# A list scheduler given the tensor engine's drain at a change of array division, and a longer assumed delay before products

## The chip, the cores and the metric

The kernel runs on one core of one Trainium2 chip. The metric is the device time of one execution in microseconds; the median of three runs stands for a kernel. The core has a tensor engine (PE in the rows; its weight loads are PEld), a vector engine (DVE), a scalar engine (ACT), GpSimd (POOL) and a queue that issues all DMAs (SP).

## The reference

One layer of a streaming encoder over 512 tokens of width 1024, in float32. Three token mixers run side by side on one input projection, their results are gated and summed, and a feed-forward block follows:

```
h = rmsnorm(x, norm_mix)
y_a = rwkv7_mixer(h @ wi[:, :OFF_HGRN], ...)          # 16 heads of 64
y_b = hgrn2_mixer(h @ wi[:, OFF_HGRN:OFF_SSM], ...)   # 8 heads of 128
y_c = mamba2_mixer(h @ wi[:, OFF_SSM:OFF_GATE], ...)  # 4 groups of 8 heads
gates = sigmoid(h @ wi[:, OFF_GATE:])                 # 3 x 1024 columns
merged = sum of gates[branch] * (y_branch @ wb[branch])
x = x + merged @ w_out
gate, up = split(rmsnorm(x, norm_ffn) @ w_ffn_in)
out = rmsnorm(x + (silu(gate) * up) @ w_ffn_out, norm_final)
```

## The kernel before

Every dense product is computed in three passes on values split into a high and a low part (`mm3`: high by high, high by low, low by high), so each weight tile that arrives by DMA is first cast by the scalar engine (`wh`, `rgh`, `gwh`) and then subtracted by the vector engine (`wl`, `rgl`, `gwl`) in `wcols`. There are three such streams: w (tiles `wr`, `wh`, `wl`), rg and gw. The normed input lies in `hh` and `hl`.

The mixers work in small pieces. The RWKV-7 mixer goes over eight pairs of heads: `r_stage1` (projections into bank `rd`, decay, the score products `SB` and `KAo`), `r_inverse` (a forward substitution of 31 steps on the vector engine, tiles `Yq` and `tmpI`, then small products) and `r_chain` (products into bank `ru`, each evacuated by the scalar or the vector engine before the next). Their products are 64 rows by 64 columns: `quads` lays four of them into quarters of the 128x128 array. The HGRN2 mixer goes over eight heads with seven levels of decay; `blocks` makes sixteen products of 128 rows by 32 columns into bank `m`. The Mamba-2 mixer works on four groups, in two streams. The gates (bank `g`, 24 tiles of 128 columns, `gates`) depend on `hh` and `hl` alone, and so do the other dense projections; these are what the tensor engine does between the pieces of the mixers. At the end `merge_early` takes two of the three branch products and `tail` does the rest: merge, output projection and feed-forward block, all in products over the full array.

What sets the order is the class `Recorder`. The kernel's instructions are not issued but recorded with what they depend on, a duration and a priority (0 RWKV chain and front, 1 next RWKV pair and all weight loads, 2 HGRN, 3 Mamba, 4 gates, 5 early merge, 6 tail). `flush` then runs a list scheduler: it steps through time, takes the engine that can start next, and gives it the instruction of the lowest priority number, and among these the first recorded, of those that are ready by then. The order found is emitted per engine (line 402 for all instructions, so rows of this kernel are told apart by tiles, not by lines). Its tables are three:

- `cost` and `passes`: durations. For a product `passes` returns the load of the weights, the passes, and which of the sixteen 32x32 parts of the array it uses; `self.pe` holds when each part has its weights and when it ends.
- `lat`: what lies between the end of one instruction and the start of one that depends on it.
- `port`, `parts`, `switch`: smaller rules for the vector and scalar engines.

Products in different parts of the array overlap in this model, and a change from full to divided use of the array costs nothing in it but the wait for the parts. The delay from a scalar or vector instruction to a product is:

```python
            if eng == "tensor":
                return 0.17 if e == "scalar" else 0.15
```

Of the kernel before, what the change touches and what calls it, by code (L numbers as in the profile page):

```python
# [74 lines left out]
class Queue:  # L75


    def __init__(self, rec, name):
        self.rec, self.name = rec, name
# [5 lines left out]
class Recorder:  # L85
# [6 lines left out]
    def __init__(self, tc):  # L92
        self.tc, self.nc = tc, tc.nc
        for e in self.ENGINES:
            if e != "gate":
                setattr(self, e, Queue(self, e))
        self.ops, self.done = [], 0
        self.prio = 0
        self.writes, self.reads, self.acc = {}, {}, {}
        self.gate, self.tiles_dram = {}, set()  # L100
        self.tiles, self.proto, self.views = [], {}, set()
        self.tags, self.prev, self.before, self.dead = {}, {}, {}, set()
        self.free = dict.fromkeys(self.ENGINES, 0.0)
        self.table = None
        self.dma = 0.0

        self.pe, self.pe_last = [[(0.0, 0.0)] * 4 for _ in range(4)], 0.0
        self.parts = {}
        self.port = {"vector": 0.0, "gpsimd": 0.0}

# [91 lines left out]
    def passes(self, out, method, args):  # L202


        n = 1
        for d in out.shape[1:]:
            n *= d
        load = args[1].shape[-1] / 1200
        if method == "transpose" or args[1].dtype == F32R:
            ps = [n / (1200 if method == "transpose" else 2226)]  # L210
        else:
            ps = [n / 1200] * 2
        rows, cols = ((q[1] // 32, -(-q[2] // 32)) for q in (self.region(args[1]), self.region(out)))
        return load, ps, [(i, j) for i in range(*rows) for j in range(*cols)]

    def shares(self, eng, method, args, kw, out):

# [84 lines left out]
    def flush(self):  # L302
        ops, lo, n = self.ops, self.done, len(self.ops)
# [4 lines left out]
        now = {e: [] for e in self.ENGINES}  # L308

        def lat(j, eng):  # L310
            e = ops[j][0]
            if e == eng:
                return {"vector": 0.13, "sync": 2.0, "tensor": -0.3}.get(e, 0.0)
            if e == "sync":
                return 1.0 if ops[j][9] > 0.5 else 2.05
            if e == "gate":
                return 0.0
            if eng == "tensor":
                return 0.17 if e == "scalar" else 0.15
            return 0.21 if e == "tensor" else 0.14  # L320

        def push(k):
# [2 lines left out]
        for k in range(n - lo):  # L325
            op = ops[lo + k]
            for j in op[5]:
                if j >= lo:
                    succ[j - lo].append(k)
                    need[k] += 1  # L330
                else:
                    ready[k] = max(ready[k], ops[j][8] + lat(j, op[0]))
            if not need[k]:
                push(k)
        order, left = [], n - lo
        while left > len(order):
# [10 lines left out]
            t, e = best  # L347
            while fut[e] and fut[e][0][0] <= t:
                k = heapq.heappop(fut[e])[1]
                heapq.heappush(now[e], (ops[lo + k][6], k))  # L350
            k = now[e][0][1]
            if e == "scalar" and self.switch(ops[lo + k]) and ops[lo + k][6] and t - ready[k] < 3:
                c = [x for x in now[e] if not self.switch(ops[lo + x[1]])]
                if c:
                    k = min(c)[1]
            now[e].remove((ops[lo + k][6], k))
            heapq.heapify(now[e])
            op = ops[lo + k]
# [3 lines left out]
                order.append(-1 - lo - k)  # L362
                left += 1
            if e == "tensor":
                load, ps, parts = op[9]
                loaded = max([ready[k]] + [self.pe[i][j][0] for i, j in parts])
                end = max(self.pe[i][j][1] for i, j in parts)
                for d in ps:
                    loaded = self.pe_last = max(loaded + load, end + 0.003, self.pe_last + 0.006)
                    end = loaded + d  # L370
                for i, j in parts:
                    self.pe[i][j] = (loaded, end)
                op[4] = end - t
# [17 lines left out]
            for m in succ[k]:  # L391
                ready[m] = max(ready[m], op[8] + lat(lo + k, ops[lo + m][0]))
                need[m] -= 1
                if not need[m]:
                    push(m)
# [1239 lines left out]
```

## Time and profile before

| | us |
|---|---|
| median of three runs | 1689.2 |
| lowest and highest run | 1685.62, 1690.41 |
| the profiled execution, whole | 1685.3 |
| its span, first to last instruction | 1683.2 |
| tensor engine busy in the span | 1645.2 |
| vector engine busy | 1021.6 |
| scalar engine busy | 832.6 |

The profiled execution is 2.1 us longer than its span and lies 3.9 us under the median of the runs. The span has two parts: up to about 1240 us the mixers with dense products between them, and from there the tail. A product's row gives its start and a duration that includes its way through the pipeline, so the distance from one start to the next tells what a product costs, and the idle time in brackets, with what ended it, is what the engine stood still. An idle time under 0.15 us is not printed.

### The profile page before, as it was taken

The numbers are of one execution on the slowest core, as the hardware profiler recorded it, in microseconds if no ns is written. First come the engines' busy times: TensorE is split into PE (matmuls) and PEld (weight loads), VectorE is DVE, ScalarE is ACT, GpSimd is POOL, SyncE is SP. The second block draws the span as 40 slices with busy tenths as digits, with TensorE's granted clock in tenths as the row PEclk, the third lists the DMA queues.
The fourth block names the chain that finished last, engine by engine and source line by source line (L and its number), as shares of the span: only waits on it lengthen the run. The fifth ranks groups of instructions, "written<-read, shape, count | busy, mean of one in ns | idle before, by whom it ended". The sixth has DMA issues, their size and how long they took to land. (4 is left out here: it accounts for less than half of the span.)

```text
span 1683.2 us, 32033 instructions
## 1 busy us (share of the span) xinstructions
PE 1645.2 (98%) x12302; PEld 1330.7 (79%) x12302; DVE 1021.6 (61%) x2327; ACT 832.6 (49%) x1518; POOL 270.3 (16%) x285
## 2 busy tenths in 40 slices
PE   7999999999999999999999999999999999999998
PEld 6887787787887777879688797777888888888886
DVE  5777878787878787884846647443353533333233
ACT  6665645657647455465755745324433433333222
POOL 1212323313223211120302103010020000000000
PEclk9999999999999999999999999999999999999999
DMA  5342333333334233433454545866572333333332
GB/s 169 80 104 62 97 80 78 78 89 78 83 74 106 70 95 82 108 89 106 124 156 118 146 126 176 280 201 202 158 219 76 113 94 94 94 94 94 96 99 75
DMA packets 291321, 192.08 MB, mean 114 GB/s; under 512 B 59054, under 2 KB 255048, under 8 KB 291168
## 3 DMA queue, kind: packets, MB, share of 16 engines
q1 hardware_dynamic: 291167, 190.04, 40.0%
q8 instruction: 96, 1.57, 0.4%
q14 instruction: 58, 0.47, 0.1%
HBM read 164.22 MB, written 25.76 MB: 113 GB/s over the span
## 5 line engine op out<-in xcount | busy, mean ns | idle before, releaser
L402 DVE TENSOR_TENSOR wl<-wr,wh 128x512 fp32r<-128x512 f32 x267 | 189.7, 711 | 244.1 <-ACT wh L402 234.9
L402 ACT CAST wh<-wr 128x512 fp32r<-128x512 f32 x267 | 164.8, 619 | 308.3 <-PE d L402 148.1
L402 DVE TENSOR_TENSOR rgl<-rgr,rgh 128x512 fp32r<-128x512 f32 x142 | 100.7, 710 | 139.0 <-ACT rgh L402 137.8
L402 ACT CAST rgh<-rgr 128x512 fp32r<-128x512 f32 x142 | 87.9, 619 | 195.6 <-PE rd L402 89.9
L402 PE MATMUL d<-hh,wh 128*128 128x512 f32 (+1 forms) x424 | 171.7, 405 | 0.4 <-DVE q L402 0.4
L402 PE MATMUL d<-hh,wl 128*128 128x512 f32 (+1 forms) x424 | 168.7, 398 | 1.1 <-DVE wl L402 1.1
L402 PE MATMUL d<-hl,wh 128*128 128x512 f32 (+1 forms) x424 | 169.0, 399 | 0.0
L402 PE MATMUL rd<-hh,rgh 128*128 128x512 f32 (+1 forms) x324 | 130.8, 404 | 3.1 <-DVE k L402 1.4
L402 PE MATMUL rd<-hh,rgl 128*128 128x512 f32 (+1 forms) x324 | 129.4, 399 | 0.0
L399 ACT ACT_TABLE_LOAD x100 | 128.3, 1283 | 1.7
L402 PE MATMUL rd<-hl,rgh 128*128 128x512 f32 (+1 forms) x324 | 129.1, 398 | 0.0
L402 PEld LDWEIGHTS d<-hh,wh 128*128 128x128 f32 x424 | 80.5, 190 | 18.0 <-issue 2.1
L402 PEld LDWEIGHTS d<-hh,wl 128*128 128x128 f32 x424 | 80.5, 190 | 17.1 <-DVE wl L402 1.4
L402 PEld LDWEIGHTS d<-hl,wh 128*128 128x128 f32 x424 | 80.7, 190 | 15.3 <-issue 1.0
L402 PE MATMUL g<-hh,gwh 128*128 128x512 f32 x192 | 77.9, 406 | 3.7 <-ACT gwh L402 3.7
L402 PEld LDWEIGHTS rd<-hh,rgh 128*128 128x128 f32 x324 | 61.1, 188 | 23.1 <-DVE k L402 4.0
L402 PE MATMUL g<-hh,gwl 128*128 128x512 f32 x192 | 78.2, 407 | 0.6 <-DVE gwl L402 0.6
L402 PE MATMUL g<-hl,gwh 128*128 128x512 f32 x192 | 77.7, 405 | 0.0
L402 POOL TENSOR_TENSOR X<-X,q 128x256 f32<-128x256 f32 x56 | 56.2, 1008 | 131.0 <-ACT X L402 110.6
L402 PE MATMUL d<-wl,hh 128*128 128x256 f32 x256 | 72.9, 285 | 0.0
L402 PEld LDWEIGHTS rd<-hh,rgl 128*128 128x128 f32 x324 | 61.0, 188 | 15.0 <-issue 1.7
L402 PE MATMUL d<-wh,hh 128*128 128x256 f32 x256 | 72.6, 285 | 0.0
(1329 smaller groups left out, 4155.2 us busy)
## 6 DMA issues: line engine op xcount, KB each, us to landing
wr<-in_w_in_dram SPq DMA_DIRECT2D x108, 256.0 KB
rgr<-in_w_in_dram SPq DMA_DIRECT2D x88, 256.0 KB
wr<-in_w_branch_dram SPq DMA_DIRECT2D x59, 256.0 KB
wr<-in_w_ffn_in_dram SPq DMA_DIRECT2D x58, 256.0 KB
gwr<-in_w_in_dram SPq DMA_DIRECT2D x96, 128.0 KB
rgr<-in_w_ffn_in_dram SPq DMA_DIRECT2D x30, 256.0 KB
wr<-in_w_ffn_out_dram SPq DMA_DIRECT2D x30, 256.0 KB
gdram<-gwr SPq DMA_DIRECT2D x24, 256.0 KB
```

What stands on the lines that cost most here:

```text
L399: self.nc.scalar.preload_act_table_set(ops[-1 - j][7])
L402: getattr(getattr(self.nc, eng), method)(*[self.resolve(x) for x in args], **{k: self.resolve(x) for k, x in kw.items()})
```

## The change

Five edits, all in the scheduler; no instruction of the kernel is added or taken away, only their order can differ.

1. The delay from a scalar or vector instruction to a product is taken as 0.37 and 0.35 us in place of 0.17 and 0.15.
2. `passes` also returns the division of a product: its rows and columns in units of 32, (4, 4) for the full array, (2, 2) for a 64x64 quarter, (4, 1) for 128 rows by 32 columns.
3. The scheduler keeps the division of the last product, `pe_mode`.
4. When a product of another division is chosen, its weights count as loaded no earlier than 0.09 us after the last product in any part has ended.
5. While the array is divided, a ready product of the same division is taken before any other, whatever its priority.

```diff
-        self.pe, self.pe_last = [[(0.0, 0.0)] * 4 for _ in range(4)], 0.0
+        self.pe, self.pe_last, self.pe_mode = [[(0.0, 0.0)] * 4 for _ in range(4)], 0.0, None
...
-        return load, ps, [(i, j) for i in range(*rows) for j in range(*cols)]
+        return load, ps, [(i, j) for i in range(*rows) for j in range(*cols)], (rows[1] - rows[0], cols[1] - cols[0])
...
             if eng == "tensor":
-                return 0.17 if e == "scalar" else 0.15
+                return 0.37 if e == "scalar" else 0.35
             return 0.21 if e == "tensor" else 0.14
...
+            if e == "tensor" and self.pe_mode not in (None, (4, 4)):
+                c = [x for x in now[e] if ops[lo + x[1]][9][3] == self.pe_mode]
+                if c:
+                    k = min(c)[1]
...
             if e == "tensor":
-                load, ps, parts = op[9]
+                load, ps, parts, mode = op[9]
                 loaded = max([ready[k]] + [self.pe[i][j][0] for i, j in parts])
                 end = max(self.pe[i][j][1] for i, j in parts)
+                if mode != self.pe_mode:
+
+                    loaded = max(loaded, max(x[1] for r in self.pe for x in r) + 0.09 - load)
+                    self.pe_mode = mode
```

The tensor engine's 9526 products stand in another order from the first to about 1240 us; the last 1597 stand as before. Along the order the division changes 390 times before and 371 times now: the array leaves its full use 176 and now 171 times, and goes from one divided use straight to another 38 and now 28 times. Ahead of the last RWKV pair's closing product (into `rs` from `sg0h`) stand 2196 products of split operands over the full array before, 102 of them into `g`, and 2118 now, 33 of them into `g`.

Three pieces show how. In all of them `g`, `d` and `rd` take dense products, `m_1573` to `m_1576` are blocks of the seventh HGRN head, `ru_1002` opens the chain of the last RWKV pair, and the first number in a name is the same in both kernels. First the tensor engine at 616 to 620 us of the profile, before:

```order
L402 MATMUL g_2243_8499<-hh_2_168,gwh_2245_8139 128x512
L402 MATMUL m_1573_8509<-X_1572_8450 32x32 x16
L402 MATMUL g_2243_8499<-hl_3_176,gwh_2245_8139 128x512
L402 MATMUL g_2243_8499<-hh_2_168,gwl_2246_8162 128x512
L402 MATMUL g_2243_8499<-hh_2_168,gwh_2248_8262 128x512
L402 MATMUL m_1576_8540<-q_1550_7098,k_1540_7081 32x32 x12
L402 MATMUL m_1575_8555<-X_1574_8482 32x32 x16
```

and, some 35 rows further, at 632 to 637 us, before:

```order
L402 MATMUL ru_935_8691<-v_930_8646,yt_934_8681 32x128 x4
L402 MATMUL g_2257_8639<-hl_3_176,gwh_2259_8632 128x512
L402 MATMUL g_2257_8639<-hh_2_168,gwl_2260_8637 128x512
L402 MATMUL ru_1002_8723<-UV_867_7855,KAo_858_7815 64x64 x16
L402 MATMUL rs_980_8746<-tmpA_981_8721,ones_42_240 128x512
L402 MATMUL rd_989_8750<-AR_977_8395,BK_978_8551 64x128
L402 MATMUL rs_980_8746<-tmpB_982_8740,ones_42_240 128x512
```

The same products now, in one piece:

```order
L411 MATMUL d_1606_8400<-hl_3_176,wh_1611_8282 128x512
L411 MATMUL m_1573_8467<-X_1572_8363 32x32 x16
L411 MATMUL m_1575_8487<-X_1574_8395 32x32 x16
L411 MATMUL ru_1002_8506<-UV_867_7511,KAo_858_7331 64x64 x16
L411 MATMUL rd_989_8530<-AR_977_8212,BK_978_8260 64x128 x8
L411 MATMUL rs_980_8545<-tmpA_981_8458,ones_42_238 128x512
L411 MATMUL ru_1003_8550<-Ot_1001_8533,SB_859_7289 64x64 x16
```

Two blocks of HGRN follow each other without a dense product between them, the chain of the pair comes straight after them, and the score products into `rd` stand together instead of one by one.

The second place is the tensor engine at 803 to 810 us, where the Mamba mixer's products `m_1851` (from `cb` and `em`) stand among the gates' products, before:

```order
L402 MATMUL m_1854_10781<-X_1841_10706,k_1742_10184 128x512
L402 MATMUL g_2257_8639<-hh_2_168,gwl_2269_10763 128x512
L402 MATMUL m_1851_10795<-em_1847_10773,cb_1843_10685 128x64 x4
L402 MATMUL g_2271_10807<-hh_2_168,gwh_2273_10797 128x512
L402 MATMUL g_2271_10807<-hl_3_176,gwh_2273_10797 128x512
L402 MATMUL g_2271_10807<-hh_2_168,gwl_2274_10809 128x512
```

and now:

```order
L411 MATMUL g_2215_5615<-hh_2_167,gwh_2226_10647 128x512
L411 MATMUL g_2215_5615<-hl_3_176,gwh_2226_10647 128x512
L411 MATMUL g_2215_5615<-hh_2_167,gwl_2227_10655 128x512
L411 MATMUL m_1851_10683<-em_1847_10602,cb_1843_10561 128x64 x4
L411 MATMUL m_1851_10683<-em_1847_10602,cb_1844_10571 128x64 x4
L411 MATMUL g_2229_10701<-hh_2_167,gwh_2231_10689 128x512
```

`m_1851` now stands behind products of the gate tile `g_2215`, which before was finished long ago, among the RWKV pairs, and its two halves stand together.

## Rows read from the trace of the kernel before

**Rows 1.** The page: span, and each engine's busy time, share and instructions.

```profile
span 1683.2 us, 32033 instructions
...
PE 1645.2 (98%) x12302; PEld 1330.7 (79%) x12302; DVE 1021.6 (61%) x2327; ACT 832.6 (49%) x1518; POOL 270.3 (16%) x285
```

**Rows 2.** Windows: stretch, length, busy us of PE, PEld, DVE, ACT, POOL; PEclk, DMA, GB/s.

```profile
40.00:1240.00 1200.00, 1180.21 (x10172) 950.09 (x10171) 831.75 (x2014) 662.19 (x1213) 254.53 (x257) 0.99 0.43 118
1240.00:1683.00 443.00, 436.57 (x1967) 356.35 (x1965) 167.19 (x263) 144.53 (x256) 10.78 (x13) 1.00 0.33 99
```

**Rows 3.** Timeline of PE: start, us, product; dense products around one block of HGRN.

```profile
408.44 0.40 PE L402 MATMUL d<-hh,wh 128*128 128x512 f32 x1
408.77 0.46 PE L402 MATMUL m<-X 128*32 128x32 f32 x32
409.16 0.50 PE L402 MATMUL d<-hl,wh 128*128 128x512 f32 x1
409.50 0.39 PE L402 MATMUL d<-hh,wl 128*128 128x512 f32 x1
409.73 0.39 PE L402 MATMUL d<-hh,wh 128*128 128x512 f32 x1
```

**Rows 4.** Timeline: two gate products and the weight load of the second.

```profile
622.54 0.39 PE L402 MATMUL g<-hh,gwh 128*128 128x512 f32 x1
622.54 0.19 PEld L402 LDWEIGHTS g<-hl,gwh 128*128 128x128 f32 x1
622.77 0.40 PE L402 MATMUL g<-hl,gwh 128*128 128x512 f32 x1
```

**Rows 5.** Waits of PE, 40 to 1240 us: total us, times, longest.

```profile
PE g L402 <- ACT gwh L402: 3.7, 4, 2.1
PE m L402 <- DVE cb L402: 1.9, 2, 1.2
PE ru L402 <- DVE SB L402: 1.8, 2, 1.5
```

**Rows 6.** Timeline of PE, 623 to 635 us; idle time before in brackets.

```profile
623.01 0.39 PE L402 MATMUL g<-hh,gwl 128*128 128x512 f32 x1
624.67 0.52 PE L402 MATMUL m<-ident,X 128*128 128x128 f32 x3 [1.27 <-DVE X L402]
...
635.10 1.15 PE L402 MATMUL ru<-UV,KAo 64*64 64x64 f32 x32 [1.50 <-DVE SB L402]
```

**Rows 7.** Timeline of PE, 803 to 808 us.

```profile
803.39 0.80 PE L402 MATMUL g<-hh,gwl 128*128 128x512 f32 x1
805.36 1.08 PE L402 MATMUL m<-em,cb 128*128 128x64 f32 x8 [1.17 <-DVE cb L402]
...
807.51 0.64 PE L402 MATMUL g<-hh,gwl 128*128 128x512 f32 x1 [0.55 <-DVE gwl L402]
807.94 0.63 PE L402 MATMUL g<-hh,gwh 128*128 128x512 f32 x1
808.37 0.63 PE L402 MATMUL g<-hl,gwh 128*128 128x512 f32 x1
```

**Rows 8.** Timeline of ACT and PE around 1099 us.

```profile
1099.42 0.40 ACT L402 CAST gwh<-gwr 128x256 fp32r<-128x256 f32 x1 [3.12 <-DMA gwr<-in_w_in_dram]
...
1099.88 0.50 PE L402 MATMUL g<-hh,gwh 128*128 128x512 f32 x1 [2.13 <-ACT gwh L402]
```

**Rows 9.** Windows of 3.4 us with half the granted clock (PEclk); columns as in Rows 2.

```profile
626.80:630.20 3.40, 3.40 (x17) 3.06 (x17) 0.95 (x3) 0.53 (x2) 0.00 (x0) 0.50 0.57 155
...
637.00:640.40 3.40, 3.40 (x57) 2.96 (x59) 3.13 (x7) 2.72 (x6) 0.00 (x0) 0.51 0.33 82
...
807.70:811.10 3.40, 3.40 (x13) 3.02 (x13) 2.35 (x6) 1.28 (x2) 0.00 (x0) 0.50 0.50 142
...
1101.30:1104.70 3.40, 3.40 (x10) 2.61 (x9) 1.25 (x3) 1.23 (x3) 0.48 (x1) 0.50 0.28 75
```

**Rows 10.** Windows: one stretch of the RWKV pairs; columns as in Rows 2.

```profile
500.00:550.00 50.00, 49.13 (x375) 38.44 (x374) 43.12 (x121) 36.36 (x64) 15.12 (x16) 1.00 0.42 108
```

## The prediction

> **What bounds the kernel now.** I read the page first [rows 1]: the tensor engine is busy 1645.2 of 1683.2 us, the vector engine 1021.6. Nothing else comes near, so the time is what the tensor engine needs, plus what it loses. The windows say where it loses [rows 2]: from 1240 us on its work lies without a gap up to the last evacuation, and the order there is the same in both kernels, so I leave that stretch out. From 40 to 1240 us it is busy 1180.2 of 1200 us, so it stands still for 19.8 us. That is all the idle time an order can win there. Busy is not the same as at its best, though, and two more losses hide inside the busy time.
>
> The first is the change of division. In the timeline [rows 3] a dense product of 512 columns starts every 0.23 us (409.50 to 409.73). A block of 32 records of HGRN products in between moves the starts from 408.44 to 409.50, with one more dense product (409.16) inside: 1.06 us, less two steps of 0.23, is 0.60 us for the block. Of that its own stream is about 0.27 us (the row's 0.46, less the some 0.20 that a single small product lasts; an estimate). So about 0.33 us goes on leaving the full array and coming back: the block starts 0.33 after the product ahead instead of 0.23, and the dense product behind it needs 0.34 to the next.
>
> The second is the clock. [...]
>
> **The change part by part.** Nothing is added or removed: 9526 products, the same evacuations, the same DMAs, three ACT table loads fewer in the order (98 for 101), off the path. Only the order up to 1240 us moves, and on all engines.
>
> (a) Changes of division, edits 2 to 5. Counted along the two orders they fall from 390 to 371: five excursions from the full array fewer (176 to 171), ten direct changes fewer (38 to 28). An excursion costs 0.33 us [rows 3]; for a direct change I take half of that, one change in place of two. 5 x 0.33 + 10 x 0.165 = 3.3 us. It lies on the path, since the engine is the bound. The bounds are 0 (the blocks only run beside each other otherwise) and 19 x 0.33 = 6.3 us; I take 3.3, by the row. The first place in the order is typical: blocks `m_1573` and `m_1575` and the chain `ru_1002` stand together, where before dense products lay between.
>
> [...] In the rows the weight load of a dense product lies beside the dense product before it, both over all 128 rows (the load starts at 622.54 with the product, the next product follows at 622.77) [rows 4]. [...]
>
> (b) The longer delay, edit 1. A product that waits starts 0.06 us after the end of what released it (the cast ends at 1099.82, the product starts at 1099.88) [rows 8]. So 0.35 us is not what the wire takes; it is a margin of 0.2 us, not quite one dense product, that the scheduler tries to fill. What can it win? Idle times in rows between 40 and 1240 us number 37 and hold about 18 us; the largest groups are the gates' casts with 3.7 us, `cb` with 1.9, `SB` with 1.8 [rows 5]. For each I counted, in both orders, the products between the last product that feeds the releaser and the product that waited, each at its steady distance. In 23 places, with 12.3 us of idle time, the distance has grown, in 6 it is the same (1.6 us), in 8, with 4.2 us, it has shrunk. `ru_1002`, which waited 1.50 us [rows 6], has two HGRN blocks ahead that it did not have; `m_1851`, which waited 1.17 us [rows 7], has another gate tile's products ahead and stands undivided. The gate product that waited 2.13 us [rows 8] is among the eight. [...] Only the last link is counted, and a releaser may be late for other reasons, so I take half: 6.1 us of the 12.3 gone, and half as much again on the eight, 2.1 us lost. That is 4.0 us won; the bounds are 12.3 won and 4.2 lost.
>
> (c) The clock. Three of the four half-clock stretches follow idle times whose distance has grown; by the same half, 1.5 stretches of 1.7 us go: 2.6 us. The bounds are 5.1 us won (three gone) and 3.4 us lost (two new).
>
> Sum: 3.3 + 4.0 + 2.6 = 9.9 us. Against the profiled execution, 1685.3 - 9.9 = 1675.4 us. That execution lies 3.9 us under the median of the runs, 1689.2, so the forecast for a median is 1679.3, in round numbers 1679 us. The best ends add to 6.3 + 12.3 + 5.1 = 23.7 us, 1665.5; the worst to 0 - 4.2 - 3.4, 7.6 us lost, 1696.8.
>
> What is queued behind a wait stays as it was: each engine takes its instructions in order, and behind a late product stand both the chain and the dense products. That is why the length of a wait counts fully.
>
> **The rivals.** *A change of division costs nothing.* If a dense product hid no load anyway, (a) would be 0 and (b) and (c) alone count: 1689.2 - 6.6 = 1682.6 us. Against it stand the 0.33 us of the row [rows 3] and the hidden load [rows 4]; I give it 0.03, and it is still faster by more than 5 us.
>
> *The waits only move.* The idle times are in part accidents: where the real run drifts from the scheduler's time, something comes late. A new order has its own accidents. Then 4.0 and 2.6 us vanish from the sum and (a) stays: 1689.2 - 3.3 = 1685.9 us. For it speaks that only 0.2 us of margin stands against waits of 1 to 2 us. Against it, that the distances have grown in 23 places of 37, most by more than the 0.2 us. That the change doesn't do what it says ends here as well: 390 changes of division to 371 is little for a rule meant to gather them, and if the drain doesn't weigh at all, the time is 1689.
>
> *The mixers become bound by the vector engine.* This one ends slower. The new order gives the tensor engine 78 dense products fewer ahead of the last RWKV pair's close (2196 to 2118), 78 x 0.23 = 18 us less to do while the eight pairs run. But the vector engine does the same substitutions and evacuations, and it is busy 43.1 of 50 us there [rows 10], 86%; only some 12 of its half-microsecond subtractions move with those products. If it can't run the pairs faster, the tensor engine stands still in the pairs for what it no longer has to do, and the products put off come later in full. At half of 18 us, with two more half-clock stretches: 9 + 3.4 - 3.3 = 9.1 us lost, 1698 us. It decides once the idle time between 40 and 1240 us is above 19.8 + 3.3, some 23 us. Against it: 14% of the vector engine is free, and the scheduler knows its durations; what it missed before was the tensor engine's loss at divisions, which made its plan too fast for that engine alone.
>
> **How the numbers follow.** About 0.3%, 5 us, is what a measurement of this kernel can tell from no change. Forecast (faster by 5 to 24 us, likeliest 10): 0.51; with the changes of division at nothing: 0.03; together 0.54 faster. Waits only move, within 5 us: 0.28. Bound by the vector engine, or accidents on the other side, slower by more than 5 us: 0.18. The range goes from the best ends, 1665, to the slower rival, 1698; below it lies 0.05, above it 0.08.
>
> **What would show it.** In the profile after: fewer products into `m` and `ru` that stand alone between dense ones, and the same 0.33 us at each that is left (a). Idle time of the tensor engine from 40 to 1240 us of some 16 us, not 20 (b), and the waits of `ru` on `SB` and of `m` on `cb` under a microsecond. Two or three half-clock stretches after 40 us, not four (c). The last pair's close (`rs` from `sg0h`) some 15 to 20 us earlier. The forecast is wrong if the idle time of the tensor engine is 20 us or more, if it lies in 150 to 650 us with the vector engine above 90% busy (the slower rival), or if half-clock stretches are as many as before in other places (the waits only move).

## The result and the profile after

The change made the kernel slower by half a percent: a median of 1696.0 us (seven runs, 1693.96 to 1698.23) against 1688.8 us (seven, 1683.13 to 1690.41), a ratio of 1.0052, interval 1.0039 to 1.0065 (the two medians divided give 1.0043). The forecast was 1679 us, with the sign the other way.

The page of the changed kernel; its execution took 1697.3 us in whole, 12.0 more than that of before. The medians differ by 7.2 only: the traced execution of before lies 3.5 us under its median and this one 1.3 above, so what follows explains the 12.0 us of two executions.

```profile
span 1695.5 us, 32048 instructions
...
PE 1648.7 (97%) x12302; PEld 1337.0 (79%) x12302; DVE 1025.3 (60%) x2327; ACT 828.9 (49%) x1515; POOL 274.6 (16%) x285
```

The tensor engine's busy time grew by 3.5 us and the span by 12.3 [rows 1]. Windows of the changed kernel, columns as in [rows 2]: the part up to the tail, the tail, and the first part in five stretches:

```profile
40.00:1252.00 1212.00, 1185.50 (x10186) 957.77 (x10185) 827.45 (x2009) 659.20 (x1210) 253.83 (x254) 0.99 0.42 115
1252.00:1695.50 443.50, 436.87 (x1968) 356.40 (x1967) 176.68 (x270) 145.36 (x258) 15.70 (x15) 1.00 0.35 104
...
40.00:150.00 110.00, 106.21 (x924) 86.03 (x924) 88.35 (x227) 69.91 (x118) 22.73 (x21) 1.00 0.36 89
150.00:300.00 150.00, 144.30 (x1585) 114.99 (x1584) 113.78 (x333) 79.63 (x145) 42.50 (x41) 0.94 0.28 71
300.00:640.00 340.00, 332.27 (x4147) 265.02 (x4147) 280.08 (x765) 201.07 (x371) 93.06 (x95) 1.00 0.33 81
640.00:900.00 260.00, 255.88 (x1899) 214.78 (x1899) 175.50 (x379) 149.39 (x278) 53.07 (x57) 1.00 0.42 115
900.00:1240.00 340.00, 334.83 (x1590) 267.24 (x1589) 166.12 (x302) 155.81 (x294) 40.80 (x41) 1.00 0.58 176
```

The same five stretches of the kernel before:

```profile
40.00:150.00 110.00, 109.30 (x1014) 86.84 (x1012) 87.39 (x227) 70.30 (x119) 25.24 (x23) 1.00 0.36 87
150.00:300.00 150.00, 147.45 (x1558) 117.27 (x1558) 117.99 (x347) 84.51 (x163) 44.16 (x43) 1.00 0.33 83
300.00:640.00 340.00, 331.90 (x4009) 264.47 (x4011) 271.94 (x758) 203.01 (x375) 89.03 (x93) 0.99 0.34 85
640.00:900.00 260.00, 256.16 (x2012) 213.59 (x2005) 176.53 (x369) 146.05 (x261) 47.09 (x49) 0.99 0.40 109
900.00:1240.00 340.00, 335.39 (x1593) 267.92 (x1593) 177.91 (x317) 158.32 (x296) 49.01 (x50) 0.99 0.60 183
```

The tail is the same (436.87 us busy of 443.50; 436.57 of 443 before). Ahead of it the tensor engine stands still for 26.5 us instead of 19.8. Length less busy time, stretch by stretch, gives 3.8, 5.7, 7.7, 4.1 and 5.2 us now and 0.7, 2.6, 8.1, 3.8 and 4.6 before. So 6.2 of the 6.7 us lie in 40 to 300 us, and the granted clock sinks there too: 0.94 in 150 to 300 us.

Windows of the changed kernel at half the granted clock:

```profile
25.90:32.70 6.80, 5.80 (x23) 5.20 (x24) 2.87 (x5) 5.13 (x8) 0.85 (x1) 0.50 0.72 204
152.20:162.40 10.20, 9.36 (x62) 7.79 (x63) 5.50 (x14) 2.10 (x5) 2.18 (x3) 0.50 0.03 4
241.00:244.40 3.40, 3.40 (x29) 2.89 (x31) 2.10 (x5) 0.97 (x2) 1.06 (x1) 0.50 0.41 100
292.20:295.60 3.40, 3.40 (x10) 2.63 (x9) 1.96 (x7) 0.00 (x0) 1.80 (x1) 0.50 0.27 72
```

The four stretches of [rows 9], at 627 to 1104 us, are gone; the forecast had one and a half of them go. In their place stand 17.0 us of half clock in 152 to 296 us (13.6 us before). The first row lies ahead of 40 us; there the kernel before has 3.4 us of half clock and 2.2 us less idle time.

Waits of the tensor engine, 40 to 1252 us of the changed kernel (total, times, longest):

```profile
PE rs L411 <- DVE KAo L411: 3.7, 2, 1.9
PE g L411 <- ACT gwr L411: 2.7, 1, 2.7
PE ru L411 <- ACT UV L411: 1.8, 3, 1.1
PE rd L411 <- ACT lf L411: 1.8, 1, 1.8
...
PE g L411 <- ACT gwh L411: 0.9, 2, 0.7
PE m L411 <- DVE cb L411: 0.9, 1, 0.9
...
PE ru L411 <- DVE SB L411: 0.6, 2, 0.3
```

The waits of [rows 5] did shrink: `gwh` 3.7 to 0.9, `cb` 1.9 to 0.9, `SB` 1.8 to 0.6. Others took their place, and the largest is new: `KAo`, twice. The timeline of the changed kernel at those two places, DVE, POOL and PE:

```profile
79.94 2.46 DVE L411 SCALAR_TENSOR_TENSOR lf<-lf,lbt,ab 128x512 f32<-128x512 f32 x1 [1.50 <-ACT ab L411]
79.94 1.90 POOL L411 TENSOR_TENSOR BK<-BK,WL 128x1024 f32<-128x1024 f32 x1 [5.63 <-PE rs L411]
82.32 0.68 DVE L411 TENSOR_TENSOR KAo<-rs,cst 128x512 f32<-128x512 f32 x1
...
83.05 0.66 PE L411 MATMUL rs<-ident,v 128*128 128x128 f32 x4 [1.78 <-DVE KAo L411]
...
148.99 1.90 POOL L411 TENSOR_TENSOR BK<-BK,WL 128x1024 f32<-128x1024 f32 x1 [4.61 <-PE rs L411]
149.05 2.75 DVE L411 TENSOR_TENSOR_SCAN cum<-one,lf 128x128 f32<-128x128 f32 x3
...
152.31 0.68 DVE L411 TENSOR_TENSOR KAo<-rs,cst 128x512 f32<-128x512 f32 x1
...
153.04 1.11 PE L411 MATMUL rs<-ident,v 128*128 128x128 f32 x4 [1.88 <-DVE KAo L411]
```

The same `lf` in the kernel before, at 79 us, where GpSimd is free, and the second place there:

```profile
79.42 0.75 DVE L402 SCALAR_TENSOR_TENSOR lf<-lf,lbt,ab 128x512 f32<-128x512 f32 x1
...
142.85 0.69 DVE L402 TENSOR_TENSOR KAo<-rs,cst 128x512 f32<-128x512 f32 x1 [0.86 <-PE rs L402]
142.90 1.90 POOL L402 TENSOR_TENSOR BK<-BK,WL 128x1024 f32<-128x1024 f32 x1 [2.04 <-PE rs L402]
143.46 1.89 DVE L402 SCALAR_TENSOR_TENSOR lf<-lf,lbt,ab 128x512 f32<-128x512 f32 x1
```

`lf` lasts 0.75 us alone and 2.46 us when it begins together with GpSimd's `BK<-BK,WL`. The end of the `rs` products releases GpSimd and makes `KAo` ready at nearly the same moment (142.90 and 142.85 us in the kernel before). Where `KAo` stands first on the vector engine (before, 142.85), `lf` pays, 1.89 us, and nobody waits for it. Where `lf` or the scans stand first (after), `KAo` comes 2.4 and 3.3 us after GpSimd's start, and the tensor engine stands for 1.8 and 1.9 us. The 2.46 us are close to 1.90 and 0.75 one after the other, 2.65.

### The profile page after: what moved, and what is told of

The parts are those of the page before. It is cut to its first block, busy times and chain, and to the rows that moved or that the text cites. A ratio compares the mean times of both kernels' runs of the same rounds, so it can differ in the third digit from the quotient of the medians.

```text
span 1695.5 us, 32048 instructions
## 1 busy us (share of the span) xinstructions
PE 1648.7 (97%) x12302; PEld 1337.0 (79%) x12302; DVE 1025.3 (60%) x2327; ACT 828.9 (49%) x1515; POOL 274.6 (16%) x285
## 4 chain that ended last, share of the span: by engine, by line
PE 77%; DVE 8%; DMA 4%; ACT 4%; issue 4%; POOL 1%; SPq 1%; POOLq 0%; DVEq 0%; ACTq 0%
PE d L411 24%; PE rd L411 15%; PE ru L411 11%; PE g L411 10%; PE rs L411 8%; PE m L411 8%; SPq L411 1%; DVE X L411 1%; ACT L408 1%; DMA em<-ydram 1%; DVE wl L411 1%; ACT ab L411 1%; DVE Yq L411 1%; DVE tmpI L411 1%; POOL gst L411 1%
## 5 line engine op out<-in xcount | busy, mean ns | idle before, releaser
L411 PE MATMUL d<-wh,hl 128*128 128x256 f32 x256 | 72.3, 283 | 0.0
```

The source lines that it names most:

```text
L411: getattr(getattr(self.nc, eng), method)(*[self.resolve(x) for x in args], **{k: self.resolve(x) for k, x in kw.items()})
```

## The experiments

Theories: **M**, the longer delay itself costs, because ready products are held back; **D**, the drain rules cost; **A**, the edits hardly matter as such, every new order has its own late arrivals and the kernel before is a good draw; and later, on the place and the mechanism, **F**, the loss comes ahead of 300 us; **V**, the vector engine becomes the bound; **G**, it comes in a stretch of the first pairs, 140 to 165 us, that is poor in dense products; **H**, it comes in the first 80 us; **P**, `KAo` comes late behind a vector instruction that GpSimd holds up; **A'**, a wait that is cured comes back elsewhere. All runs compare with the kernel before on the same chip, by ratio.

### One edit alone, and one step of 0.01 us

`delay_only` is the kernel before with edit 1, `drain_only` the changed kernel without it; `before_d18` and `after_d36` move the delay by 0.01 us.

```diff
 delay_only (in the kernel before)
-                return 0.17 if e == "scalar" else 0.15
+                return 0.37 if e == "scalar" else 0.35
 drain_only (in the changed kernel)
-                return 0.37 if e == "scalar" else 0.35
+                return 0.17 if e == "scalar" else 0.15
 before_d18 (in the kernel before)
+                return 0.18 if e == "scalar" else 0.16
 after_d36 (in the changed kernel)
+                return 0.36 if e == "scalar" else 0.34
```

> The kernel before with edit 1 alone: 0.37 and 0.35 us from scalar and vector instructions to products, no drain, no preference for the same division. Along its order the division changes 413 times (390 before, 371 after); 2048 dense products stand ahead of the last pair's close (2196 before, 2118 after). Theory M (the margin costs: with the longer delay the scheduler puts the RWKV chain ahead of dense work, and the tensor engine then waits for the vector engine): about 1696 us or more, since still fewer dense products stand ahead; idle time of the tensor engine from 40 us to the tail well above 20 us. Theory D (the drain and the preference cost): about 1689 us, as before. Theory A (any new order has its own accidents): anywhere from 1682 to 1700.

> The changed kernel with the old delay of 0.17 and 0.15 us: edits 2 to 5 alone. 369 changes of division, 2139 dense products ahead of the last close. Theory M: about 1686 us, as before less some 3 us for 21 changes of division. Theory D: about 1696 us, as the changed kernel. Theory A: anywhere from 1682 to 1700.

> The kernel before with 0.18 and 0.16 us in place of 0.17 and 0.15: 0.01 us more in one table, nothing else. It moves the order as far as the change does: 406 changes of division for 390, 2176 dense products ahead of the last close for 2196. Theories M and D: within 0.2% of before, 1686 to 1692 us, since a twentieth of the margin can do no more. Theory A: as far off as the change, by 5 us or more, most likely slower, since the kernel before is the one of its kind that was kept.

> The changed kernel with 0.36 and 0.34 us in place of 0.37 and 0.35. 365 changes of division, 2131 dense products ahead of the last close. Theories M and D: as the changed kernel, 1693 to 1699 us. Theory A: off by several us to either side; faster than before is as possible as slower than the change.

Measured: 1.0112 (1.0091 to 1.0133), 1.0056 (1.0034 to 1.0078), 1.0034 (1.0021 to 1.0047) and 1.0008 (0.9988 to 1.0027). Each half of the change is slower than before, and the two don't add: 1.1% and 0.6% alone, 0.5% together. One step of 0.01 us costs 0.3% in one kernel and gives back 0.4% in the other, nearly what the whole change costs. That speaks for A; what M has left is that edit 1 alone is the worst of all.

Waits of the tensor engine in `delay_only`, 640 to 900 us:

```profile
PE m L402 <- DVE X L402: 3.8, 3, 2.7
PE m L402 <- DVE tmpI L402: 2.9, 1, 2.9
PE rd L402 <- DVE bv L402: 1.3, 2, 0.8
```

In the kernel before the largest in that stretch is `cb` [rows 5]. Its loss lies elsewhere, then: 12.4 us of idle time in 640 to 900 us, where the changed kernel has 4.1.

### Half by half, and the drain's two parts

`late_only` applies the change's rules from 300 us of the scheduler's own time on, `early_only` up to there; `pref_only` has edit 5 alone, `cost_only` edit 4 alone, both with the old delay.

```diff
 late_only (early_only: < 300.0)
-                return 0.37 if e == "scalar" else 0.35
+                d = 0.2 if ops[j][8] >= 300.0 else 0.0
+                return d + (0.17 if e == "scalar" else 0.15)
...
-            if e == "tensor" and self.pe_mode not in (None, (4, 4)):
+            if e == "tensor" and t >= 300.0 and self.pe_mode not in (None, (4, 4)):
...
-                    loaded = max(loaded, max(x[1] for r in self.pe for x in r) + 0.09 - load)
+                    if t >= 300.0:
+                        loaded = max(loaded, max(x[1] for r in self.pe for x in r) + 0.09 - load)
```

> The rules of the change (longer delay, drain, preference) hold only from 300 us of the scheduler's time on; the order is that of the kernel before up to 318 us of its trace. Theory F (the change loses its time early: idle time of the tensor engine up to 300 us grew from 7.3 to 17.2 us and the half-clock stretches there from 3.4 to 23.8 us, while from 300 us on it is no worse): idle up to 300 us 7 to 8 us, no half-clock stretch between 40 and 300 us, total 1680 to 1686 us, faster than both. Theory A (any new order meets its own late arrivals, and that before is one of the lucky ones): new idle events of 1 to 3 us behind 320 us with half-clock stretches after them, total 1689 to 1697 us.

> The mirror: the rules of the change hold up to 300 us of the scheduler's time, the old ones behind; the order is that of the changed kernel up to 323 us of its trace. Theory F: it has the changed kernel's early loss and no gain behind it, 1696 to 1702 us. Theory A: the early part costs its 10 to 13 us, and the rest is a new draw of late arrivals, anywhere from 1690 to 1705 us, so this run alone doesn't tell; with the other half it does: under F the two differences from the kernel before add up to that of the change (+7 us), under A they don't.

> The kernel before with the preference for the present division alone (no drain in the scheduler's times, old delay): 377 changes of division, 13 fewer than before, 2187 dense products ahead of the last pair's close (2196 before). Theory D (the preference is right, it is the scheduler's view of a drain or of the delay that costs): the 13 changes times 0.165 to 0.33 us are won, 1684.5 to 1686.5 us. Theory A: 1686 to 1698 us, whatever the changes of division do, with new idle events of over 1 us.

> The kernel before with the drain in the scheduler's times alone (no preference, old delay): 393 changes of division, 2061 dense products ahead of the last pair's close, 135 fewer than before. Theory V (the slower rival of the prediction: products put off behind the pairs that the vector engine can't run faster): last close less than 15 us earlier though 135 x 0.23 = 31 us of products are gone from ahead of it, idle time spread over 150 to 650 us, 1698 us or more. Theory A: 1688 to 1700 us, with the loss in a few idle events of over 1 us and half-clock stretches behind them, and a last close some 25 us earlier.

Measured: `late_only` 0.9999 (0.9989 to 1.0008), `early_only` 1.0078 (1.0061 to 1.0095), `pref_only` 1.0039 (1.0024 to 1.0054), `cost_only` 1.0091 (1.0076 to 1.0106). On the place these two are as F says: the new rules behind 318 us cost nothing, ahead of it they cost more than the whole change. But behind the switch each is a new order, and two single orders can fall so under A too; and `late_only` isn't faster than before, as F wanted. Its new waits behind 318 us (22.3 us of idle time in 40 to 1252 us) take what its clock gives (10.2 us of half clock in that stretch for 13.6). V, the vector engine as the bound, isn't what `cost_only` shows: its last pair closes 18.7 us earlier in the trace (732.7 against 751.4), though not by the 31 us of products gone, the vector engine is busy 397.9 of 500 us in 150 to 650 us, 80%, and 6.8 of its 8.8 us of extra idle time lie in 40 to 150 and 640 to 900 us.

A warning came with these traces. In the changed kernel the tensor engine waits 3.1 us for `wh` near 27 us, and 1.4 us before. Waits up to 40 us in `late_only`, whose tensor engine still has the order of before there:

```profile
PE ru L412 <- ACT wh L412: 3.1, 1, 3.1
```

So this part of the difference between two profiled executions isn't the order. In the traces of seventeen of the twenty kernels this wait is 2.7 to 3.4 us; the trace of before is one of three with 1.4 to 1.8.

### Bands

The same condition for 0 to 70 us (`band_a`), 70 to 175 (`band_b`), 175 to 300 (`band_c`), and everywhere but 70 to 175 (`hole_b`). I thought that the place was 140 to 165 us. There the changed kernel's tensor engine runs 17 us of small products with almost no dense one between them (14 dense products start in 140 to 170 us, 45 before), and the clock is halved for 10.2 us.

> The rules of the change hold only up to 70 us of the scheduler's time; the tensor engine's order is that of the changed kernel up to 83 us of its trace, and the scheduler goes on by the old rules. Theory G (the change's early loss lies in the dry stretch of the first pairs, 140 to 165 us: the rules draw the dense products together ahead of it, so that the chain's small products stand alone, their waits are open and the clock falls; in the driest 12 us of work there stand 6 dense products in the changed kernel, 9 here and before): no half-clock stretch between 140 and 165 us, total 1686 to 1692 us. Theory H (the loss comes in the first 80 us, where the tensor engine waited 3.1 us for wh and 1.8 us for KAo): half-clock or not, 1693 us or more.

> The rules hold only from 70 to 175 us of the scheduler's time; the order is that of the kernel before up to 77 us of its trace. In the driest 12 us of work of the first pairs stand 3 dense products (before 9, changed kernel 6). Theory G: a half-clock stretch of 6 us or more between 140 and 165 us, 4 to 8 us lost there, total 1692 to 1698 us. Theory H: as before, 1686 to 1690 us.

> The rules hold only from 175 to 300 us of the scheduler's time; the order is that of the kernel before up to 191 us of its trace. 9 dense products in the driest 12 us of the first pairs, as before. Theory G: no half-clock stretch between 140 and 165 us and none of the change's early loss: 1686 to 1692 us. A third reading (the loss lies in the second pair, where the changed kernel has half-clock stretches at 241 and 292 us): 1693 us or more.

> The changed kernel with the old rules from 70 to 175 us of the scheduler's time; the order is that of the changed kernel up to 83 us of its trace. 9 dense products in the driest 12 us of the first pairs. Theory G: the half-clock stretch of 10.2 us and the wait of 1.9 us for KAo at 153 us are gone, total 1686 to 1690 us, 6 to 10 us under the changed kernel. Theory H: 1694 to 1698 us, as the changed kernel. Theory A (any order draws its own accidents): anywhere from 1687 to 1700 us, with its losses in other places than those named.

Measured: 1.0060 (1.0043 to 1.0077), 1.0026 (1.0013 to 1.0039), 1.0040 (1.0020 to 1.0060), 1.0085 (1.0061 to 1.0109). G falls: `hole_b`, with the old rules in its place, is the slowest of the four, and `band_b`, the poorest in dense products by the count in its expectation, has no half-clock stretch there. What the half clock near 150 us goes with in these four is the beginning. `band_a` and `hole_b` share the changed kernel's order up to 83 us, and both have its wait for `KAo` at 82 us (1.6 and 1.5 us), a second one of 1.8 us behind 130 us, and half clock for 10.2 and 13.7 us from 148 and 147 us on. The three kernels with the order of before up to at least 77 us (`late_only`, `band_b`, `band_c`) have no half clock in 130 to 320 us. The beginning isn't all, though: `band_c` begins like before and loses 0.4%, a time that its third reading named, but not in the second pair, where that reading put it. Its idle time in 150 to 300 us is 2.4 us (before 2.5), and its extra lies in 640 to 900 us, 9.3 us against 3.8.

### The beginning, and the one instruction

`late70` has the change from 70 us of the scheduler's time on. `swap2` is the changed kernel with one vector instruction in another place, for each of the first two pairs; every other engine's order is untouched. `d36_swap` is that cure on `after_d36`, where it finds only the first place.

```diff
 swap2: DVE, first pair
+KAo<-rs,cst
 lf<-lf,lbt,ab
-KAo<-rs,cst
 swap2: DVE, second pair
+KAo<-rs,cst
 cum<-one,lf
 cum<-one,lf
 cum<-one,lf
 X<-X,k
-KAo<-rs,cst
```

> The rules of the change from 70 us of the scheduler's time on, the old ones up to there; the order is that of the kernel before up to 77 us of its trace. Theory H (the part of the loss that all orders with the changed kernel's beginning share comes from the order up to 83 us: at the first pair's close they are 7 to 10 us behind at the same work): first close of the eight pairs at 173 to 178 us, no wait of over 1 us for KAo near 80 us, total 1686 to 1692 us. Theory A (each order draws its own, the beginning doesn't matter): 1688 to 1702 us, and a first close at 180 us or more.

> The changed kernel with its whole order, but for one instruction of the vector engine that stands earlier at two places: the last evacuation KAo<-rs,cst of the first pair ahead of lf<-lf,lbt,ab (one instruction earlier), that of the second pair ahead of three scans cum<-one,lf and X<-X,k (four earlier). All other engines' orders are the changed kernel's. Theory P (in the changed kernel the vector engine's instruction ahead of KAo starts with GpSimd's BK<-BK,WL of 1.90 us and lasts until that ends, and the tensor engine waits 1.78 and 1.88 us behind it): both waits for KAo fall under 0.3 us; if the half-clock stretch of 10.2 us at 152 us comes from the second wait it goes too, 1.8 + 1.9 + 5 us: 1687 to 1689 us. If the half-clock stretch comes from the small products alone it stays: 1692 to 1693 us. Theory A' (the wait moves to what stands behind the instructions put later): 1695 to 1697 us, with a new wait of over 1 us within 10 us behind each place.

> The changed kernel with a delay of 0.36 and 0.34 us, which measured 1.0008 of before, and the first pair's last KAo<-rs,cst ahead of lf<-lf,lbt,ab on the vector engine. Theory P: its wait of 1.8 us for KAo at 82 us and the half-clock stretch of 3.4 us that begins there (82.3 us) go, 1.8 + 1.7 us: 0.998 to 0.999 of before, 1684 to 1686 us, faster than both kernels by a little. Theory A': 1.000 to 1.002.

Measured: `late70` 1.0013 (1.0001 to 1.0025): without its first 70 us the change costs next to nothing, and with them alone (`band_a`) it costs all of it. That is as H says. But H is not enough: `after_d36` and `after_d38` begin like the changed kernel too, the tensor engine's order being the same up to 127 and 139 us at least, and have the same wait of 1.78 us for `KAo` at 82 us. They end level with before. So a beginning doesn't fix the time. `swap2` 1.0045 (1.0033 to 1.0057): by the intervals not distinct from the changed kernel's 1.0052. `d36_swap` 0.9999 (0.9986 to 1.0012), faster than neither kernel.

The close of the first pair shows what the beginning costs by then, since nearly the same work lies ahead of it (510 to 519 dense products). In order: before, changed kernel, `swap2`, `after_d36`, `d36_swap`:

```profile
175.43 0.40 PE L402 MATMUL rs<-sg0h,gh 128*128 128x512 f32 x1
185.55 0.50 PE L411 MATMUL rs<-sg0h,gh 128*128 128x512 f32 x1 [0.58 <-DVE y L411]
178.76 0.50 PE L421 MATMUL rs<-sg0h,gh 128*128 128x512 f32 x1 [0.58 <-DVE y L421]
182.09 0.40 PE L411 MATMUL rs<-sg0h,gh 128*128 128x512 f32 x1
174.41 0.40 PE L421 MATMUL rs<-sg0h,gh 128*128 128x512 f32 x1
```

The six kernels that begin like the changed one close it at 178.6 to 185.6 us, the five that begin like before at 173.8 to 176.1 (`late70` 175.1, where H wanted it). The changed kernel is 10.1 us behind, and the cure brings back 6.8 us in `swap2` and 7.7 in `d36_swap`, one execution each. The early loss is there, then, and most of it goes with these one or two places. The whole time hardly shows it: `after_d36` is 6.7 us behind here and ends level with before.

The timeline of `swap2` at the two places:

```profile
78.33 0.69 DVE L421 TENSOR_TENSOR KAo<-rs,cst 128x512 f32<-128x512 f32 x1 [1.46 <-PE rs L421]
78.38 1.90 POOL L421 TENSOR_TENSOR BK<-BK,WL 128x1024 f32<-128x1024 f32 x1 [5.63 <-PE rs L421]
78.94 1.89 DVE L421 SCALAR_TENSOR_TENSOR lf<-lf,lbt,ab 128x512 f32<-128x512 f32 x1
...
79.54 0.60 PE L421 MATMUL rs<-ident,v 128*128 128x128 f32 x4
...
146.02 1.90 POOL L421 TENSOR_TENSOR BK<-BK,WL 128x1024 f32<-128x1024 f32 x1 [4.62 <-PE rs L421]
146.09 0.68 DVE L421 TENSOR_TENSOR KAo<-rs,cst 128x512 f32<-128x512 f32 x1
146.69 2.15 DVE L421 TENSOR_TENSOR_SCAN cum<-one,lf 128x128 f32<-128x128 f32 x3
...
148.13 0.66 PE L421 MATMUL rs<-ident,v 128*128 128x128 f32 x4
```

The mechanism is as P says: `KAo` now starts with GpSimd, `lf` and the scans pay (1.89 and 2.15 us; in the kernel before `lf` takes 0.75 us and a scan 0.41 where GpSimd is idle), and neither `rs<-ident,v` waits. The time is not: P wanted 1687 to 1693 us, and 1.0045 of 1688.8 us is 1696.4. The windows of `swap2`:

```profile
40.00:150.00 110.00, 107.00 (x976) 87.11 (x977) 89.47 (x231) 69.59 (x118) 23.44 (x21) 1.00 0.36 89
150.00:300.00 150.00, 146.56 (x1585) 116.88 (x1583) 115.85 (x340) 85.11 (x162) 43.41 (x44) 0.99 0.31 78
300.00:640.00 340.00, 331.32 (x4185) 263.88 (x4186) 278.44 (x766) 199.04 (x368) 93.24 (x95) 1.00 0.31 79
640.00:900.00 260.00, 255.16 (x1845) 214.64 (x1846) 177.64 (x381) 150.80 (x275) 50.88 (x57) 1.00 0.41 117
900.00:1240.00 340.00, 333.54 (x1576) 266.82 (x1575) 159.45 (x290) 152.39 (x287) 39.07 (x38) 1.00 0.57 175
```

Up to 300 us its idle time is 6.4 us against 9.5 in the changed kernel. Behind, with the tensor engine's very same order, it is 20.0 against 17.0. In these two executions, then, the 3.1 us won early come back later as other waits. That is A' in its time but not in its sign, a new wait of over 1 us within 10 us behind each place: the longest there is 0.69 us, `m` on `X` at 149.5 us. The half clock near 150 us shrank from 10.2 to 3.4 us in this execution, which, at 1689.5 us, is the fastest of its six; I don't build on it.

### Neighbours

`before_d14` and `before_d22` are the kernel before with 0.14 and 0.22 us, `after_d38` the changed kernel with 0.38 (each 0.02 less for vector operations).

> The kernel before with an assumed delay of 0.14 and 0.12 us in place of 0.17 and 0.15. Theory M (the longer the assumed delay, the more ready products are held back, and that is what costs): not slower than before, 0.998 to 1.001. Theory A (each value draws an order with its own late arrivals; the value of the kernel before is one of the good draws): 1.002 to 1.008, with the difference in idle time and clock and not in the changes of division, which are 390 in both.

> The kernel before with 0.22 and 0.20 us: 407 changes of division for 390. Theory M: between 0.18 us (1.0034) and 0.37 us (1.0112), 1.004 to 1.007. Theory A: anywhere from 1.001 to 1.008. A price for the changes of division alone, 17 x 0.17 to 0.33 us: 1.002 to 1.003.

> The changed kernel with 0.38 and 0.36 us in place of 0.37 and 0.35: 370 changes of division (371). Its neighbour with 0.36 us measured 1.0008, the changed kernel itself 1.0052. Theory M: 1.005 to 1.006. Theory A: anywhere from 1.000 to 1.009.

Measured: 1.0036 (1.0022 to 1.0051), 1.0057 (1.0037 to 1.0077), 1.0011 (0.9994 to 1.0028). With the old rules the delays 0.14, 0.17, 0.18, 0.22 and 0.37 give 1.0036, 1, 1.0034, 1.0057 and 1.0112; with the new ones 0.17, 0.36, 0.37 and 0.38 give 1.0056, 1.0008, 1.0052 and 1.0011. Under the new rules the time jumps either way, as A says. Under the old ones it also grows from 0.18 us on, as M says, but M can't explain 0.14.

All twenty orders, each by its profiled execution: idle time of the tensor engine in 40 to 1252 us, half-clock time from 40 us to the tail, changes of division, whole time, and the ratio of the timed runs:

| kernel | idle us | half clock us | changes | profiled us | ratio |
|---|---|---|---|---|---|
| before | 19.8 | 13.6 | 390 | 1685.3 | 1 |
| d36_swap | 20.6 | 10.2 | 365 | 1684.0 | 0.9999 |
| before_d18 | 21.7 | 17.0 | 406 | 1690.7 | 1.0034 |
| late_only | 22.3 | 10.2 | 384 | 1689.6 | 0.9999 |
| band_b | 23.1 | 10.2 | 385 | 1690.0 | 1.0026 |
| band_a | 23.1 | 17.0 | 397 | 1696.0 | 1.0060 |
| after_d36 | 23.4 | 23.8 | 365 | 1693.6 | 1.0008 |
| before_d22 | 24.1 | 20.4 | 407 | 1697.0 | 1.0057 |
| drain_only | 24.5 | 17.1 | 369 | 1695.7 | 1.0056 |
| after_d38 | 24.8 | 6.8 | 370 | 1686.6 | 1.0011 |
| early_only | 25.1 | 17.0 | 398 | 1697.3 | 1.0078 |
| before_d14 | 25.2 | 10.2 | 390 | 1691.8 | 1.0036 |
| band_c | 26.1 | 3.4 | 405 | 1693.7 | 1.0040 |
| swap2 | 26.4 | 3.4 | 371 | 1689.5 | 1.0045 |
| the change | 26.5 | 17.0 | 371 | 1697.3 | 1.0052 |
| pref_only | 26.7 | 13.6 | 377 | 1696.1 | 1.0039 |
| late70 | 26.8 | 17.0 | 373 | 1694.8 | 1.0013 |
| hole_b | 27.8 | 20.5 | 379 | 1697.9 | 1.0085 |
| cost_only | 28.6 | 20.4 | 393 | 1702.7 | 1.0091 |
| delay_only | 31.1 | 23.8 | 413 | 1706.3 | 1.0112 |

A least-squares fit over these rows gives the profiled time as 1623 us + 1.30 x idle + 0.42 x half clock + 0.084 x changes. The twenty times scatter by 5.4 us (standard deviation), by 4.9 once changes of division alone are fitted, by 1.9 with idle time and half clock, by 1.5 with all three. So what a traced execution costs is its idle time and its clock, which is near to bookkeeping. The timed ratios say less: in us of 1687 they scatter by 5.3 us, and the same two columns leave 3.2 of that. In these single traces the kernel before has the least idle time of all, and no order beat it.

## Why the prediction was wrong, point by point

**What bounds it, and where the losses hide: right.** The tensor engine's order decides, the tail didn't move, and idle time and clock leave a scatter of 1.9 us in 20 traced executions.

**(a) Changes of division, 3.3 us: right in kind, too large by a quarter to a factor of two.** By the fit the 19 changes fewer are worth 19 x 0.084 = 1.6 us. Added up over each trace, at the changes ahead of which the engine didn't stand still the next product starts later than the steady distance of the product ahead would have it, by 51.5 us in 379 changes before and 48.1 us in 352 now. That is 0.14 us each, 2.6 us for 19. The rival that a change of division costs nothing isn't borne out. The rows have a dense product's load, 0.19 us, beside the dense product ahead, from that product's start on [rows 4]. Divisions are a small part of what tells orders apart: of the 21 us between before and `delay_only` the 23 changes more are 2 us by the fit.

**(b) The longer delay, 4.0 us won: this is the step that failed.** For the largest waits of the old order the direction was right: `gwh`, `cb` and `SB` fell from 7.4 to 2.4 us, by more than the half that was taken. But it looked only at waits that the old order had. A new order has waits that no row of the old trace can show, and the sum had no term for them; only the second rival had. The four largest groups alone, `KAo`, `gwr`, `UV` and `lf`, came to 10.0 us, of which the kernel before has 0.5. The bound of 4.2 us lost was therefore too narrow: the idle time grew by 6.7. And even the largest new waits, the two for `KAo`, aren't in the product order at all. They hang on what stands in front on the vector engine, one instruction at the first place and four at the second, and on GpSimd starting with it, which a count of products ahead can't see.

**(c) The clock, 2.6 us won: failed for the same reason.** No row shows the 1.7 us a stretch as such. A window of [rows 9] lasts 3.4 us, and in the one at 807.7 us dense products start 0.43 us apart [rows 7], against 0.23 at 409.50 us [rows 3], so half its length is an estimate. The stretches of [rows 9] went, and 17.0 us of half clock came at 152 to 296 us for 13.6. At half its length the difference is 1.7 us lost, inside the bounds, where 2.6 us were to be won.

In the two traces, then: 6.7 us of idle time and 1.7 of clock from 40 us on, 2.2 of idle time and 1.7 of clock up to there, less 1.6 to 2.6 us of divisions. That is 10 to 11 of the 12.0 us.

**The rivals.** "The waits only move" had the mechanism, `swap2` even shows waits moving with the tensor engine's order held fixed, but its time, 1685.9 us, took the new waits to be as many as the old ones. They were more in 19 orders of 19, by one trace each. The slower rival, 1698 us, was near in time and wrong in the mechanism. Half of the new idle time, 3.4 of 6.7 us, does lie in its 150 to 650 us, but the vector engine is busy 398.6 of 500 us there (399.9 before), 80% and not above 90%. In 500 to 550 us it has 43.3 us of work as before [rows 10], and idle time in 300 to 640 us fell. Its threshold, 23 us of idle time, was passed at 26.5 us all the same. The last close came 5.5 us earlier (745.9 against 751.4), not 15 to 20. The sign given in the list of what would show it, idle time of 20 us or more, is what decided.

**What stays open.** Shown, in one trace each: the changed kernel's excess is idle time and clock, most of it comes in the first 300 us, and up to the close of the first pair it goes with the kernel's beginning. Shown for two waits, 3.7 us: how they arise. Not shown: which order's waits make the measured half percent. The beginning alone doesn't (`after_d36` and `after_d38` share it and end level with before; `late70` against `band_a` are two single orders), and curing the two waits gave 0.07% with an uncertainty of about 0.2%. Nor do the runs tell whether a longer delay is bad in itself (0.18, 0.22, 0.37 us under the old rules) or drew badly three times. Under the new rules 0.36 and 0.38 us are level with before, so the change as made is partly an unlucky draw of its own family, and a lucky one would have been no gain.

## What to carry to other kernels

In a list schedule that is already nearly full, an edit of the scheduler's costs is a draw among orders: before crediting or blaming the edit, move its constant by a hair either way, and take the spread (here 0.4%) as its uncertainty. Counting which old waits go gives only half of the sum; the new order's waits aren't in the old trace, and 19 of 19 new orders had more idle time than a kernel whose order had little. A cheap way to find the place of a loss is to switch the new rules on and off by the scheduler's own time, since the order up to the switch is that of one of the two kernels. Behind the switch every order is a new draw, so the time of such a run alone doesn't settle the place; a milestone ahead of which the work is the same, here the close of the first pair, does better.

## What the runs showed of the hardware

- The vector instruction `lf<-lf,lbt,ab`, started together with GpSimd's `BK<-BK,WL` of 1.90 us, took 2.46 instead of 0.75 us, while the evacuation `KAo<-rs,cst` beside the same GpSimd instruction took 0.68 to 0.69 us, and 0.68 without it. The cost fell on what stood behind `lf` in the vector engine's order: in the changed kernel `KAo`, from 82.32 us on, and the tensor engine waited 1.78 us for it.
- Runs of one and the same kernel differ along with the clock: over 234 runs, each within its kernel and batch, 0.001 less of the mean granted clock goes with 1.2 us more (correlation -0.71), and the runs scatter by 2.4 us. Single profiled executions lay up to 7 us off their kernel's median (`late70`: 1694.8 against 1687.9), which is as much as the change itself.
- Half clock came without a long stop ahead of it: in `cost_only` the clock is 0.50 for 10.2 us from 147.4 us on, and in 130 to 147 us the longest wait is 0.6 us and the engine is busy for 15.5 us. In `band_b` a wait of 1.5 us for `KAo` among the first pairs' small products, in 130 to 165 us, is followed by no half clock up to 320 us.
